# Weight sums of the last down projection moved into the second up projection, and gates by ScalarE's Silu

## The chip, the cores and the metric

The kernel runs on one core of a Trainium2 chip. A core has a matrix engine (TensorE, PE in the profile, its weight loads PEld), a vector engine (VectorE, DVE), a scalar engine for activation functions (ScalarE, ACT), a general engine (GpSimd, POOL) and an engine that issues transfers (SyncE, SP). SyncE, ScalarE and GpSimd can each issue DMA transfers. The metric is the time of one execution on the device in microseconds; the median of three runs is compared.

## The reference

The computation is a trunk of two layers on 512 tokens of width 1024, in float32. Each layer has a token mixer with three branches (an RWKV-7 recurrence, a chunked retention and a spatial gating unit), whose outputs are gated, summed and projected, and then a gated MLP with a causal convolution of width 3. A final RMSNorm ends it. The change touches the MLP only:

```python
def conv_ffn(h, w_up, conv_w, conv_b, w_down):
    S = h.shape[1]
    u = h @ w_up                                   # 1024 -> 2 x 2816
    up = jnp.pad(u, ((0, 0), (CONV_WIDTH - 1, 0), (0, 0)))
    c = conv_b
    for j in range(CONV_WIDTH):
        c = c + conv_w[j] * up[:, j:j + S]
    gate, val = jnp.split(c, 2, axis=-1)
    return (jax.nn.silu(gate) * val) @ w_down      # 2816 -> 1024

...
for l in range(DEPTH):                             # DEPTH = 2
    ...                                            # the mixer
    x = x + conv_ffn(rmsnorm(x, norm2_g[l]), ffn_w_up[l], ffn_conv_w[l], ffn_conv_b[l], ffn_w_down[l])
return rmsnorm(x, final_g)
```

## The kernel before

**Products.** Every large product is made of matmuls of 128x128 weights with 128x512 activations. For accuracy each operand is split into a high and a low part (`part` and `split`, lines 130 to 150: ScalarE copies the high part, line 139 or 148; VectorE subtracts, line 140 or 149), and each product takes three matmuls (`mm3`, line 152, issued at line 156). A unit of weights is 128x512, 256 KB. `load` (line 121) fetches units on SyncE's queue a few units ahead, in the order that a first pass over the program noted.

**Order.** The program is written once, in program order. A scheduler then orders each engine's instructions by their priority, which follows program order, and by a simulated time line. An instruction marked by `keep_in_program_order` is pinned behind the instruction that was written before it for the same engine. Each engine and each queue works in order, so an instruction that waits holds up those behind it. Tiles come from pools with a fixed number of buffers; a tile waits until the buffer's last user is done.

**Up projection (`ffn_up`, line 1058).** It makes 44 columns of 128 in pairs, column i for the gate and column 22 + i for the value, i from 0 to 21. One column is two units of weights and 24 matmuls into one of four accumulators (`acc`). VectorE takes the accumulator out with the norm's factor (line 1082, tile `fu`). ScalarE makes the first tap with the bias (line 1084), VectorE the other two (lines 1085 and 1086). For each pair ScalarE then makes a Tanh of half the gate (line 1090), and VectorE two products (lines 1091 and 1092), so the result is twice silu(gate) times the value; the factor of one half is applied behind the down projection. In layer 0 the result is split for the matmuls. In layer 1 `halves` (line 1101) combines each two results with four half-size VectorE instructions and two splits, and GpSimd's queue stores parts of it to DRAM (lines 1108, 1109, 1113). In layer 1 GpSimd's queue also turns the residual (line 1076) in the odd steps i below 17. The first three columns are computed before the norm's factor is known (`firstF`).

**Down projections.** Layer 0's (`ffn_down`, line 1117) makes 8 rows of 66 matmuls each. Layer 1's (`last`, line 1134) uses a seven-product scheme on 2x2 blocks. Four of the seven products need sums and differences of the four 128x512 blocks of a quad of weights; there are 11 quads, q = 0 to 10. It first goes through the quads with the products 4 to 7, 24 matmuls a quad, then through the products 1, 2 and 3.

**The weight sums (`presum`, line 237).** A quad is four loads on GpSimd's queue (line 253, tiles `pre` from tensor `wdt`), four VectorE subtractions or additions (lines 242 to 245) and four stores to DRAM (line 248, tensor `ts`), from where `load` reads them back in the last down projection. The table `PRE` says where a quad is loaded; it is summed at the next call. Quads 0 to 3 are loaded in layer 0's up projection at i = 2, 4, 6 and 8 into 16 tiles of the pool of activations (`fpre`), and quads 4 to 10 in layer 0's down projection, one for each of its first seven rows, into tiles of the general pool `u`. So all sums are done before layer 1 begins.

## Time and profile before

| | us |
|---|---|
| median of three runs | 1702.77 |
| lowest and highest run | 1701.46, 1706.15 |
| the profiled execution | 1701.58 |
| its span, first to last instruction | 1699.7 |
| TensorE busy in the span | 1687.0 |
| VectorE busy | 1233.1 |
| ScalarE busy | 799.9 |
| GpSimd busy | 240.8 |

The profile is of one execution. Its times are counted from the first instruction; the 1.9 us between its own time and its span lie before and behind. Matmuls are pipelined: each is listed with a length of some 390 ns, while the next starts earlier, so the pace has to be read from starts. VectorE and ScalarE overlap back-to-back instructions a little as well. A wait is put down to the instruction that released it. The line of an instruction is that of the statement, which can be in a helper; line 156 stands for almost all matmuls. Tiles are named without their numbers: `sh`, `sl` and `wh`, `wl` are the high and low parts of weights, `ah` of activations, `wr` the raw weights.

### The profile page before, as it was taken

What the parts mean: (1) busy time and instruction counts of PE and PEld (TensorE: products, weight loads), DVE (VectorE), ACT (ScalarE), POOL (GpSimd) and SP (SyncE); (2) the same over time, 40 slices, a digit from 0 to 9 for tenths busy, and PEclk for the clock granted to TensorE, in tenths of its full rate; (3) what the DMA queues carried; (4) which work ended last, traced back from release to release, by engine and by line L of the source; (5) the groups of instructions that cost most, each with busy time, mean ns of one, the idle gap of its engine ahead of it and who ended that gap; (6) DMA issues with size and microseconds to landing.
All of it is one profiled execution on the core that took longest, in us unless ns stands there. A gap on an engine that the chain in (4) does not pass through costs nothing.

```text
span 1699.7 us, 27885 instructions
## 1 busy us (share of the span) xinstructions
PE 1687.0 (99%) x10214; PEld 1379.7 (81%) x10214; DVE 1233.1 (73%) x2157; ACT 799.9 (47%) x1367; POOL 240.8 (14%) x336
## 2 busy tenths in 40 slices
PE   9999999999999999999999999999999999999998
PEld 7888777888888888888888888777888888887786
DVE  6887746578669887655568888455775698888776
ACT  6563433554355444433355644335542554444565
POOL 2121000003301200003321210000132022110000
PEclk9999999999999999999999999999999999999999
DMA  5236552524544532147743365525254443433774
GB/s 182 87 108 203 177 179 94 181 92 161 189 146 147 194 123 95 63 145 260 255 142 100 97 211 172 180 94 188 85 173 149 155 136 132 130 131 112 241 243 167
DMA packets 147768, 260.01 MB, mean 153 GB/s; under 512 B 19600, under 2 KB 39952, under 8 KB 147632
## 3 DMA queue, kind: packets, MB, share of 16 engines
q1 hardware_dynamic: 122960, 192.87, 35.2%
q0 software_dynamic: 15888, 49.95, 8.7%
q10 hardware_dynamic: 8784, 15.42, 2.6%
q8 instruction: 80, 1.31, 0.3%
q14 instruction: 56, 0.46, 0.1%
HBM read 212.94 MB, written 45.22 MB: 152 GB/s over the span
## 4 chain that ended last, share of the span: by engine, by line
PE 90%; DVE 4%; DMA 3%; issue 1%; ACT 1%; SPq 0%; ACTq 0%; DVEq 0%
PE acc L156 82%; PE sm L156 3%; PE sm L664 2%; DVE wl L140 1%; DMA wr<-wall 1%; PE sm L917 1%; PE sm L571 1%; DMA tr<-bkT 1%; DVE sl L140 0%; PE sm L1022 0%; ACT wh L139 0%; DVE cs L790 0%; DMA wr<-ts 0%; DVE TMP L788 0%; DMA x<-xT 0%
## 5 line engine op out<-in xcount | busy, mean ns | idle before, releaser
L156 PE MATMUL acc<-lo,sh 128*128 128x512 f32 x1108 | 431.8, 390 | 0.5 <-ACT sh L139 0.5
L156 PE MATMUL acc<-hi,sh 128*128 128x512 f32 x1108 | 431.9, 390 | 0.0
L156 PE MATMUL acc<-hi,sl 128*128 128x512 f32 x1108 | 430.3, 390 | 0.2 <-DVE sl L140 0.2
L139 ACT CAST sh<-wr 128x512 fp32r<-128x512 f32 (+1 forms) x375 | 228.3, 615 | 370.3 <-PE acc L156 217.6
L140 DVE TENSOR_TENSOR sl<-wr,sh 128x512 fp32r<-128x512 f32 (+1 forms) x375 | 254.5, 684 | 103.5 <-ACT sh L139 78.3
L140 DVE TENSOR_TENSOR wl<-wr,wh 128x512 fp32r<-128x512 f32 x238 | 166.5, 703 | 144.5 <-ACT wh L139 141.1
L139 ACT CAST wh<-wr 128x512 fp32r<-128x512 f32 x238 | 146.8, 619 | 244.4 <-PE acc L156 160.3
L156 PEld LDWEIGHTS acc<-lo,sh 128*128 128x128 f32 x1108 | 208.0, 188 | 45.0 <-ACT sh L139 1.2
L156 PEld LDWEIGHTS acc<-hi,sl 128*128 128x128 f32 x1108 | 208.0, 188 | 44.1 <-DVE sl L140 0.7
L156 PEld LDWEIGHTS acc<-hi,sh 128*128 128x128 f32 x1108 | 208.0, 188 | 43.1 <-issue 0.3
L156 PE MATMUL acc<-lo,wh 128*128 128x512 f32 x588 | 232.3, 395 | 0.3 <-DVE lo L215 0.2
L156 PE MATMUL acc<-hi,wl 128*128 128x512 f32 x588 | 229.8, 391 | 0.5 <-DVE wl L140 0.5
L156 PE MATMUL acc<-hi,wh 128*128 128x512 f32 x588 | 229.3, 390 | 0.0
L156 PEld LDWEIGHTS acc<-lo,wh 128*128 128x128 f32 x588 | 110.5, 188 | 25.5 <-DVE lo L215 1.5
L156 PEld LDWEIGHTS acc<-hi,wl 128*128 128x128 f32 x588 | 110.4, 188 | 25.4 <-DVE wl L140 1.5
L156 PEld LDWEIGHTS acc<-hi,wh 128*128 128x128 f32 x588 | 110.6, 188 | 22.5 <-issue 0.2
L156 PE MATMUL acc<-ah,sh 128*128 128x512 f32 x352 | 108.4, 389 | 0.0
L1084 ACT ACTIVATE cv<-fu,pc 128x512 f32<-128x512 f32 x88 | 71.6, 816 | 61.1 <-DVE fu L1082 59.8
L1082 DVE TENSOR_TENSOR fu<-acc,rsF 128x512 f32<-128x512 f32 x88 | 60.6, 688 | 39.8 <-PE acc L156 39.7
L156 PE MATMUL acc<-wl,hi 128*128 128x512 f32 x212 | 86.1, 406 | 0.0
L156 PE MATMUL acc<-wh,lo 128*128 128x512 f32 x212 | 82.8, 391 | 0.0
L156 PE MATMUL acc<-wh,hi 128*128 128x512 f32 x212 | 82.7, 390 | 0.0
(359 smaller groups left out, 2426.8 us busy)
## 6 DMA issues: line engine op xcount, KB each, us to landing
wr<-wall SPq DMA_DIRECT2D x488, 256.0 KB, 2.8
gd<-gth ACTq DMA_DIRECT2D x48, 256.0 KB, 3.0
gth<-gd POOLq DMA_DIRECT2D x48, 256.0 KB, 3.5
pre<-wdt POOLq DMA_DIRECT2D x44, 256.0 KB, 5.9
ts<-pre POOLq DMA_DIRECT2D x44, 256.0 KB, 2.8
wr<-ts SPq DMA_DIRECT2D x44, 256.0 KB, 3.9
wr<-wdn SPq DMA_DIRECT2D x40, 256.0 KB, 4.2
wr<-wdt SPq DMA_DIRECT2D x33, 256.0 KB, 3.6
```

The costliest lines, as they stand in the source:

```text
L139: self.kept(self.nc.scalar.copy(hi[:, :n], raw[:, :n]))
L140: self.kept(self.nc.vector.tensor_tensor(lo[:, :n], raw[:, :n], hi[:, :n], op=SUB))
L156: i = self.nc.tensor.matmul(*x, **y, **kw)
L571: i = T.matmul(pK[hv[1 - h], j, :], bk[hv[h], c, 1, :], x[hv[h], c, :], start=True, stop=True)
L664: po(T.matmul(o, l, r, start=start, stop=True, skip_group_check=True))
L917: po(T.matmul(X[h][:, i, :], lhsT, rhs, start=new[h], stop=stop, skip_group_check=True))
L1082: V.tensor_tensor(u, ps, self.rsF, op=MUL)
L1084: A.activation(t, u, AF.Identity, scale=self.p("cw2", j), bias=self.p("cb", j))
```

## The change

All eleven quads move into layer 1. A generator `sums` makes one quad in four steps: issue its four loads; nothing; two sums with their two stores; the other two sums with theirs. All of these are pinned in program order on VectorE and on GpSimd's queue. `presum` advances the generator by one step and does something in layer 1 only: after each column of the up projection with i below 20, after the first column of i = 20 (41 steps), and after the quads q = 0, 1 and 2 of the first pass of `last` (3 steps). So ten quads are done in the up projection; the eleventh is loaded at i = 20 and summed in `last`.

The tiles `pre` get a pool of their own with six buffers, four for a quad, so that two loads of the next quad find a free buffer and the other two wait for stores. [...] The 16 tiles of `fpre` and the 28 tiles of `u` are no longer taken in layer 0.

In both up projections ScalarE makes Silu of the gate in place of Tanh of half of it, and one VectorE instruction (twice silu, times the value) takes the place of two.

```diff
-PRE = {(0, "f", 2): 0, (0, "f", 4): 1, (0, "f", 6): 2, (0, "f", 8): 3, (0, "d", 0): 4, (0, "d", 1): 5, (0, "d", 2): 6, (0, "d", 3): 7,
-       (0, "d", 4): 8, (0, "d", 5): 9, (0, "d", 6): 10}
+RING = 4096
...
+        self.pp = tp("pp", 6)
...
-    def presum(self, l, stage, m):
...
+    def sums(self, l):
+
+        P, V, po = self.nc.gpsimd, self.nc.vector, self.tc.keep_in_program_order
+        for q in range(NFF // 2):
+            b = [self.pp.tile([128, 512], F32, name=self.nm("pre"), tag="pre") for _ in range(4)]
             for i, t in enumerate(b):
-                self.nc.gpsimd.dma_start(t, self.a["wdt"][0, 2 * q + i // 2][:, i % 2 * 512:i % 2 * 512 + 512])
-            self.pre.append((q, b))
+                po(P.dma_start(t, self.a["wdt"][l - 1, 2 * q + i // 2][:, i % 2 * 512:i % 2 * 512 + 512]))
+            yield
+            yield
+            for p, o, x, op in ((7, 3, 1, SUB), (5, 1, 0, SUB), (6, 0, 3, ADD), (4, 2, 0, SUB)):
+                po(V.tensor_tensor(b[o], b[o], b[x], op=op))
+                self.tsum[l, q, p] = self.dp.tile([128, 512], F32, name=self.nm("ts"))
+                po(P.dma_start(self.tsum[l, q, p], b[o]))
+                if p == 5:
+                    yield
+            yield
+
+    def presum(self, l):
+        if l == L - 1:
+            next(self.sum, None)
...
         first = self.firstF(l, (78, 79, 80), st, (3,))
-        if l == 0:
-            self.fpre = [[self.f(n="pre") for _ in range(4)] for _ in range(4)]
+        self.sum = self.sums(l)
         for i in range(NFF):
-            if l == 0 and i % 2 == 0 and 2 <= i <= 10:
-                self.presum(l, "f", i)
...
                 cs.append(t)
+                if i < 20 or i == 20 and j == i:
+                    self.presum(l)
             g, v = cs
             th = self.u(n="fth")
-            A.activation(th, g, AF.Tanh, scale=0.5)
-            V.scalar_tensor_tensor(th, th, 1.0, g, op0=ADD, op1=MUL)
-            V.tensor_tensor(th, th, v, op=MUL)
+            A.activation(th, g, AF.Silu)
+            V.scalar_tensor_tensor(th, th, 2.0, v, op0=MUL, op1=MUL)
...
-            self.presum(l, "d", m)
...
+            if q < 3:
+                self.presum(L - 1)
...
-        nc = _bacc.Bacc("TRN2", target_bir_lowering=False, num_devices=1)
+        nc = _bacc.Bacc("TRN2", target_bir_lowering=False, num_devices=1, dynamic_dma_scratch_size=RING)
```

More of the change, by code (lines that the diff above doesn't have):

```diff
@@ L123, in load @@
         raw = self.u(n="wr") if u[5] == "q" and self.nraw % 2 else self.wp.tile([128, 512], F32, name=self.nm("wr"), tag="wr", bufs=NRAW)
-        src = self.tsum[i] if name == "tsum" else self.a[name][l, i]
+        src = self.tsum[(l, *i)] if name == "tsum" else self.a[name][l, i]
         with self.tc.high_priority():
@@ L235, in trip @@
         return d
-    def presum(self, l, stage, m):
-        if self.pre:
-            q, b = self.pre.pop()
-            V = self.nc.vector
-            V.tensor_tensor(b[3], b[3], b[1], op=SUB)
-            V.tensor_tensor(b[1], b[1], b[0], op=SUB)
-            V.tensor_tensor(b[0], b[0], b[3], op=ADD)
-            V.tensor_tensor(b[2], b[2], b[0], op=SUB)
-            for p, t in zip((7, 5, 6, 4), (b[3], b[1], b[0], b[2])):
-                self.tsum[q, p] = self.dp.tile([128, 512], F32, name=self.nm("ts"))
-                self.nc.gpsimd.dma_start(self.tsum[q, p], t)
-        q = PRE.get((l, stage, m))
-        if q is not None:
-            b = self.fpre.pop(0) if stage == "f" else [self.u(n="pre") for _ in range(4)]
-            for i, t in enumerate(b):
-                self.nc.gpsimd.dma_start(t, self.a["wdt"][0, 2 * q + i // 2][:, i % 2 * 512:i % 2 * 512 + 512])
-            self.pre.append((q, b))
+    def sums(self, l):
+        P, V, po = self.nc.gpsimd, self.nc.vector, self.tc.keep_in_program_order
+        for q in range(NFF // 2):
+            b = [self.pp.tile([128, 512], F32, name=self.nm("pre"), tag="pre") for _ in range(4)]
+            for i, t in enumerate(b):
+                po(P.dma_start(t, self.a["wdt"][l - 1, 2 * q + i // 2][:, i % 2 * 512:i % 2 * 512 + 512]))
[11 more added lines that the diff above has]
+            next(self.sum, None)
     def norm_new(self):
@@ L326, in run @@
         self.con = self.cp.tile([128, NCC], F32, name="con")
-        self.pre, self.tsum = [], {}
+        self.tsum = {}
         self.rst = self.cp.tile([128, 512], F32, name="rst")
@@ L1144, in unit @@
             if p > 3:
-                return self.unit("tsum", 0, (q, p), 0)
+                return self.unit("tsum", L - 1, (q, p), 0)
             return self.unit("wdt", 0, 2 * q + (p > 1), 512 * (p == 3))
```

## The prediction

> **What bounds the kernel now.** I read the head of the page first, then the busy time by stretch, then the chain in order of time.

> ```profile
> span 1699.7 us, 27885 instructions
> PE 1687.0 (99%) x10214; PEld 1379.7 (81%) x10214; DVE 1233.1 (73%) x2157; ACT 799.9 (47%) x1367; POOL 240.8 (14%) x336
> PE 90%; DVE 4%; DMA 3%; issue 1%; ACT 1%; SPq 0%; ACTq 0%; DVEq 0%
> ```

> TensorE is busy for 99% of the span, so other work costs time only where it makes TensorE wait. The stretches that the change touches, from the view of busy time by stretch (after the length: PE, PEld, DVE, ACT, POOL busy with instruction counts, TensorE clock, DMA share, GB/s):

> ```profile
> 509.00:752.00 243.00, 243.00 (x1074) 201.28 (x1073) 196.36 (x310) 113.94 (x177) 15.03 (x28) 1.00 0.37 123
> 530.00:620.00 90.00, 90.00 (x399) 74.55 (x398) 79.96 (x127) 43.60 (x69) 15.03 (x28) 1.00 0.52 179
> 752.00:866.00 114.00, 114.00 (x505) 94.42 (x504) 61.14 (x97) 36.45 (x63) 34.35 (x64) 1.00 0.74 248
> 980.00:1142.00 162.00, 161.78 (x1785) 129.14 (x1785) 107.28 (x217) 65.60 (x118) 17.89 (x17) 1.00 0.52 167
> 1142.00:1262.00 120.00, 119.29 (x643) 98.27 (x639) 83.04 (x163) 59.84 (x111) 18.81 (x23) 1.00 0.44 143
> 1360.00:1380.00 20.00, 20.00 (x90) 16.56 (x89) 19.70 (x32) 11.41 (x17) 3.85 (x7) 1.00 0.41 133
> 1357.00:1572.00 215.00, 214.49 (x946) 176.93 (x944) 186.23 (x307) 100.67 (x157) 35.62 (x65) 1.00 0.39 128
> 1380.00:1560.00 180.00, 180.00 (x795) 149.02 (x794) 155.37 (x259) 83.61 (x132) 30.70 (x56) 1.00 0.39 129
> 1572.00:1600.00 28.00, 27.18 (x116) 21.46 (x116) 21.70 (x37) 13.20 (x23) 2.70 (x5) 1.00 0.62 190
> 1600.00:1620.00 20.00, 20.00 (x90) 16.52 (x90) 14.38 (x23) 12.81 (x24) 0.00 (x0) 1.00 0.96 330
> ```

> The first up projection is 509 to 752, the first down projection 752 to 866, the second up projection 1357 to about 1590, the last down projection after it. A busy PE can still be a slowed PE, so I checked the pace in the chain in order of time (start, length, what, count):

> ```profile
> 509.76 355.19 PE acc L156 x1567
> 1357.30 210.36 PE acc L156 x928
> ```

> 355.19/1567 and 210.36/928 both give 0.2267 us for one matmul. With VectorE 81% busy and 87% busy, with the sums there and without, TensorE steps at the same pace. A column (24 matmuls) is 5.44 us. The instructions of TensorE that waited between 1568 and 1606 (idle time in brackets):

> ```profile
> 1570.87 0.50 PE L156 MATMUL acc<-lo,sh 128*128 128x512 f32 x1 [0.51 <-ACT sh L139]
> 1572.35 0.50 PE L156 MATMUL acc<-hi,sl 128*128 128x512 f32 x1 [0.22 <-DVE sl L140]
> 1592.53 0.50 PE L156 MATMUL acc<-wl,ah 128*128 128x512 f32 x1 [0.41 <-DVE wl L140]
> 1598.78 0.50 PE L156 MATMUL acc<-sl,ah 128*128 128x512 f32 x1 [0.16 <-DVE sl L140]
> ```

> Together 1.30 us, always for the split of a weight. This seam between the second up projection and the last down projection is the only place under the change where TensorE waits for VectorE.

> **Part 1: the sums leave layer 0.** Removed there: 44 loads, 44 stores and 44 VectorE instructions.

> ```profile
> L242 DVE TENSOR_TENSOR pre<-pre,pre 128x512 f32<-128x512 f32 x11 | 7.6, 690 | 15.8 <-DMA pre<-wdt 15.8
> L248 POOL DMA_DIRECT2D ts<-pre x44 | 23.9, 542 | 194.8 <-DVE pre L242 169.3 <-DVE pre L245 8.4 <-DVE pre L243 6.0
> L253 POOL DMA_DIRECT2D pre<-wdt x44 | 23.4, 539 | 0.0
> ```

> and from the view of waits (in all, times, longest):

> ```profile
> DVE pre L242 <- DMA pre<-wdt: 15.8, 6, 3.3
> ```

> VectorE gets back 44 x 0.69 = 30 us and 15.8 us of waiting, GpSimd's queue 47 us of issues. All of it lies beside TensorE, which is full in both stretches (243.00 of 243, 114.00 of 114), so I take 0. What can follow is another order in layer 1's mixer. There TensorE's recorded idle is 0.22 + 0.71 us, the end below: -0.9. For the end above, compare the two layers' mixers, whose neighbours differ already:

> ```profile
> 199.21 1.27 PE sm L808 x83
> 414.55 1.42 PE sm L972 x13
> 1045.45 1.27 PE sm L808 x83
> 1261.37 1.42 PE sm L972 x13
> ```

> From L808 to L972 it is 215.34 us in layer 0 and 215.92 us in layer 1. The end above is +0.6.

> **Part 2: the sums and the gates in the second up projection.** One call a column makes one quad (four loads, four sums, four stores) every four columns, 21.8 us. Ten quads fit, the eleventh is loaded there and summed after q = 1 and 2 of the last down projection. Silu drops one VectorE instruction per gate.

> ```profile
> L1091 DVE SCALAR_TENSOR_TENSOR fth<-fth,cv 128x512 f32<-128x512 f32 x44 | 30.1, 684 | 0.2 <-ACT fth L1090 0.2
> L1090 ACT ACTIVATE fth<-cv 128x512 f32<-128x512 f32 x44 | 27.2, 618 | 0.5 <-DVE cv L1086 0.3
> ```

> VectorE: + 40 x 0.69 = 27.6, - 22 x 0.684 = 15.0, so +12.6 us over 44 columns, 0.29 us a column. In 1380 to 1560 VectorE was idle 24.6 us in 33 columns, 0.75 a column. That leaves 0.46 a column, about 20 us in the stage: VectorE goes from 86% to 92%. The nearest rows: in 530 to 620 VectorE had four quads and was 89% busy, and from 1360 to 1380 98%, and TensorE was full in both. I take 0; below nothing is to be had, since TensorE is full from 1380 to 1560; the end above is the first rival. In layer 0 the 22 dropped instructions are hidden by the same full TensorE.

> The DMA issues (count, size, median us from issue to landing):

> ```profile
> pre<-wdt POOLq DMA_DIRECT2D x44, 256.0 KB, 5.9
> ts<-pre POOLq DMA_DIRECT2D x44, 256.0 KB, 2.8
> wr<-wdn SPq DMA_DIRECT2D x40, 256.0 KB, 4.2
> ```

> GpSimd: 80 issues x 0.54 = 43 us more beside the 35.62 of 215 us now, so its queue has room; its order matters more. The loads of a quad are pinned behind the last store of the gates before, the sums two columns (10.9 us) after the call. Four issues and the landing (5.9 us) take 8.1 us, so they arrive in time by some 3 us, less when a store ahead of them waits for VectorE. Each store waits for its sum, and the next gate's two stores, for which L1114 waits, stand behind it; VectorE comes to the sum first, in the same order.

> The bus: 80 x 0.262 MB in 239 us is 88 GB/s on top of 128, together 216. In the first down projection it was 248 GB/s with the weights landing after 4.2 us, and TensorE full. Nothing.

> The smaller descriptor ring: the trace shows no wait for room. From below it is 0; from above, one more landing (5.9 us) per quad, which makes the sums 3 us late (first rival). Four loads were issued 0.54 us apart without a wait, so few are in flight, and I take 0. [...]

> Table loads of ScalarE, at the Tanh of the gates and at the Gelu of the mixer:

> ```profile
> L1090 ACT ACT_TABLE_LOAD x2: 1283/1283/1283, 518.6 to 1366.1; - x2
> L1004 ACT ACT_TABLE_LOAD x2: 1283/1283/1283, 334.6 to 1180.8; - x2
> ```

> Tanh had one per layer, after the Sqrt of the norm; Silu needs one too. If Silu's table lacked the copies of L139 and the Identity of L1084, each gate would cost two reloads, 22 x 2 x 1.28 = 56 us of ScalarE, 157 of 215 us.

> Tanh and Gelu ran among those copies with one load per stage, so I take 0. [...]

> **Part 3: the seam.** The last two gates give VectorE back 2 x 0.68 = 1.4 us. The eleventh quad puts in 4 x 0.69 = 2.8 us, in pairs, pinned between weight splits for which TensorE already waits, so a pair can be paid in full: net +1.4. Its four stores are 1.05 MB, 3.2 us of the bus at 330 GB/s, just before the loads of 1600 to 1620 (share 0.96), with TensorE full there. Ends: -1.3 (all four waits go) and 1.4 + 3.2 = +4.6. I take +1.4, since each recorded wait ends with a split and not with a load.

> **Sum.** 0 + 0 + 1.4. The profiled execution took 1701.58 us (span 1699.7 and 1.9 around it) and becomes 1703.0. It lies 1.2 below the median of 1702.77, so the median goes to 1704.2 us. About 0.3% (5.1 us) is what a measurement here tells from no change, as the three runs spread from 1701.46 to 1706.15.

> **Rivals.**
> Slower, VectorE falls behind in the second up projection: 6 of the 11 quads waited for their loads now, 15.8 us, 2.6 each, the longest 3.3 (the row of waits above). If all eleven wait, that is 29 to 36 us; about 20 are free, and TensorE pays 9 to 16: 1712 to 1719. It decides from 20/11 = 1.8 us a quad. For it: loads of one quad behind gate stores that wait for VectorE. Against: the 3 us in hand and the 89% row. An issue took 0.54 us, sixteen of them in the stretch where VectorE was 89% busy. [...]
> Slower, the seam pays bus and sums: 4.6 or more, 1707.4 and up, beyond 0.3% if a further split is late.
> Silu reloads tables at each gate: the splits queue behind 1.28 us loads; TensorE pays up to 56 us, 1759.
> Faster, the waits go: all of TensorE's recorded idle in 980 to 1262 and 1357 to 1600 is 0.22 + 0.71 + 0.51 + 0.82 = 2.3 us, 1700.5, still within 0.3%. More would need the end of the kernel, which the change doesn't touch.

> **How the numbers follow.** My forecast and the small gain, both within 0.3%: 0.71. VectorE behind: 0.13. The seam beyond 0.3%: 0.06. Tables: 0.03. Faster by over 0.3%, by a cause that I don't see: 0.07. So faster 0.07, same 0.71, slower 0.22. The range runs from 1700 (the gain, and the spread of runs) to 1712, where the first rival begins; left out are that rival, the tables and part of the faster case, about 0.2. Within the forecast alone it is 1701 to 1707.

> **What would show it.** Right: the pace stays 0.2267 in both long pieces of the chain; VectorE near 92% in 1380 to 1560; no wait for `pre` over 1 us; ten table loads; TensorE's waits at the seam 1 to 3 us in all. Wrong: waits of PE for `sh`, `sl` or accumulators inside the second up projection, long waits of VectorE for `pre` or of GpSimd for slots, or a mixer of layer 1 that differs by more than 1 us.

## The result, and the profile after

The changed kernel takes 1710.38 us (median of six runs, 1707.74 to 1711.77), the kernel before 1704.35 us on the same chip (1701.46 to 1706.15). The ratio is 1.0031, with a 95% interval from 1.0021 to 1.0042: slower by about 5.3 us, just at the bound of 0.3% that the prediction had set. The profiled execution took 1709.89 us, with a span of 1708.2 us against 1699.7. The head of its page:

```profile
span 1708.2 us, 27807 instructions
PE 1690.1 (99%) x10214; PEld 1382.0 (81%) x10214; DVE 1209.2 (71%) x2113; ACT 799.6 (47%) x1367; POOL 240.8 (14%) x336
PE 79%; DVE 7%; DMA 5%; issue 5%; ACT 2%; POOL 1%; SPq 1%; ACTq 0%; DVEq 0%; POOLq 0%
```

TensorE still fills 99% of the span, but the chain that ended last runs over it for 79% in place of 90%. From here on lines behind 240 are a few higher or lower than in the kernel before (L1081 takes the accumulator out, L1083 to L1085 make the taps, L1091 the Silu, L243, L247 and L249 load, add and store the sums).

Rows of the chain in order of time (start, length, what), by which the two executions can be laid side by side:

```profile
415.01 1.42 PE sm L974 x13
510.25 355.19 PE acc L156 x1567
1045.94 1.27 PE sm L810 x83
1262.67 1.42 PE sm L974 x13
1358.58 41.42 PE acc L156 x183
```

The changed kernel is 0.46 us late at the end of layer 0's mixer (415.01 against 414.55) and 0.49 late at 1045.94. So from layer 0's up projection, which has the same unbroken piece of 1567 matmuls in 355.19 us, to the start of layer 1 nothing was won or lost. Layer 1's mixer adds 0.8 (1.30 late at 1262.67), and the second up projection begins 1.28 late. The end is 8.5 late, so about 7.2 us are lost from the second up projection on. Its unbroken piece of 928 matmuls is cut down to 183. The busy time by stretch (after the length: PE, PEld, DVE, ACT, POOL busy, TensorE clock, DMA share, GB/s):

```profile
752.00:866.00 114.00, 114.00 (x505) 94.45 (x504) 43.36 (x69) 36.62 (x63) 4.33 (x8) 1.00 0.41 119
1380.00:1560.00 180.00, 178.64 (x785) 146.88 (x784) 158.60 (x268) 79.16 (x129) 67.83 (x126) 1.00 0.70 225
1577.00:1584.00 7.00, 6.44 (x16) 5.08 (x17) 3.26 (x6) 2.17 (x4) 1.11 (x3) 0.55 0.85 296
```

TensorE's waits between 1380 and 1610, and its matmuls behind the longest (idle time in brackets):

```profile
1496.68 0.50 PE L156 MATMUL acc<-lo,sh 128*128 128x512 f32 x1 [1.20 <-ACT sh L139]
...
1577.56 0.80 PE L156 MATMUL acc<-lo,sh 128*128 128x512 f32 x1 [3.57 <-ACT sh L139]
1578.15 0.63 PE L156 MATMUL acc<-hi,sh 128*128 128x512 f32 x1
1578.58 0.63 PE L156 MATMUL acc<-lo,sh 128*128 128x512 f32 x1
...
1582.85 0.63 PE L156 MATMUL acc<-hi,sh 128*128 128x512 f32 x1
...
1584.01 0.40 PE L156 MATMUL acc<-hi,sh 128*128 128x512 f32 x1
1584.24 0.39 PE L156 MATMUL acc<-hi,sl 128*128 128x512 f32 x1
...
1604.08 0.50 PE L156 MATMUL sm<-wl,ah 128*128 128x512 f32 x1 [0.34 <-DVE wl L140]
```

The waits are 5.1 us, against 1.30 before. Behind the wait of 3.57 us the matmuls come 0.43 us apart (1578.15, 1578.58, ...) and only by 1584 are they 0.23 apart again: the clock row says 0.55 there. From 1578.15 to 1582.85 eleven steps took 4.70 us where 2.49 was the pace, so these steps alone lost 2.2 us to the slow clock. The waits' 3.8 us more than before and these 2.2 make 6.0 of the 7.2 us; the rest lies in single long steps behind the first wait, near 1531 and at the edges of the slow stretch. About a third was lost early: from 1380 to 1560 ten matmuls fewer were made than before (785 against 795), which is 2.3 us at 0.2267 each. The mean granted clock was 0.997 or 0.998 in all six executions and 0.999 in the profiled one of the kernel before, so the others lost clock as well; where, their records do not show.

Why was `sh`, a cast of weights on ScalarE, late? Waits in 1380 to 1560, first of the kernel before, then of the changed one (in all, times, longest):

```profile
ACT sh L139 <- PE acc L156: 50.2, 38, 2.6
DVE fu L1082 <- PE acc L156: 10.0, 15, 1.6
ACT sh L139 <- DMA wr<-wall: 7.4, 3, 4.0
DVE sl L140 <- ACT sh L139: 1.7, 1, 1.7
```

```profile
ACT sh L139 <- DMA wr<-wall: 33.9, 18, 4.7
DVE sl L140 <- ACT sh L139: 15.2, 6, 4.2
ACT sh L139 <- PE acc L156: 6.8, 2, 4.7
DVE fu L1081 <- PE acc L156: 0.4, 1, 0.4
DVE pre L247 <- DMA pre<-wdt: 0.3, 1, 0.3
```

Before, VectorE and ScalarE waited for TensorE (10.0 and 50.2 us): both were ahead. After, VectorE hardly ever waits for TensorE (0.4 us): it runs behind. It does not wait for the blocks of the sums (0.3 us). It waits 15.2 us for ScalarE's casts (1.7 before), and those wait 33.9 us for weights to land. The weight loads issued in this stretch, before and after (count, size, median us from issue to landing):

```profile
wr<-wall SPq DMA_DIRECT2D x63, 256.0 KB, 2.6
wr<-wall SPq DMA_DIRECT2D x61, 256.0 KB, 3.6
```

### The profile page after: what moved, and what is told of

Same layout as the page of the kernel before. It is cut to its first block, busy times and chain, and to the rows that moved or that the text cites. A ratio compares the mean times of both kernels' runs of the same rounds, so it can differ in the third digit from the quotient of the medians.

```text
span 1708.2 us, 27807 instructions
## 1 busy us (share of the span) xinstructions
PE 1690.1 (99%) x10214; PEld 1382.0 (81%) x10214; DVE 1209.2 (71%) x2113; ACT 799.6 (47%) x1367; POOL 240.8 (14%) x336
## 4 chain that ended last, share of the span: by engine, by line
PE 79%; DVE 7%; DMA 5%; issue 5%; ACT 2%; POOL 1%; SPq 1%; ACTq 0%; DVEq 0%; POOLq 0%
PE acc L156 70%; PE sm L156 3%; PE sm L666 2%; DMA wr<-wall 2%; DVE sl L140 1%; PE sm L919 1%; DVE wl L140 1%; PE sm L573 1%; DVE fu L1081 1%; DVE pre L247 1%; DVE cv L1084 1%; DMA tr<-qkt 1%; POOL pre L243 0%; DVE cv L1085 0%; PE sm L1024 0%
## 5 line engine op out<-in xcount | busy, mean ns | idle before, releaser
L156 PE MATMUL acc<-lo,sh 128*128 128x512 f32 x1108 | 433.7, 392 | 4.8 <-ACT sh L139 4.8
L156 PE MATMUL acc<-hi,sh 128*128 128x512 f32 x1108 | 433.6, 391 | 0.0
L156 PE MATMUL acc<-hi,sl 128*128 128x512 f32 x1108 | 432.0, 391 | 0.2
L139 ACT CAST sh<-wr 128x512 fp32r<-128x512 f32 (+1 forms) x375 | 227.9, 615 | 334.0 <-PE acc L156 204.2
L140 DVE TENSOR_TENSOR sl<-wr,sh 128x512 fp32r<-128x512 f32 (+1 forms) x375 | 255.1, 685 | 147.0 <-ACT sh L139 88.7
L140 DVE TENSOR_TENSOR wl<-wr,wh 128x512 fp32r<-128x512 f32 x238 | 166.8, 703 | 137.7 <-ACT wh L139 132.7
L139 ACT CAST wh<-wr 128x512 fp32r<-128x512 f32 x238 | 146.7, 619 | 241.4 <-PE acc L156 158.1
L156 PEld LDWEIGHTS acc<-lo,sh 128*128 128x128 f32 x1108 | 208.8, 188 | 49.4 <-ACT sh L139 5.8
L156 PEld LDWEIGHTS acc<-hi,sl 128*128 128x128 f32 x1108 | 208.7, 188 | 44.9 <-DVE sl L140 0.9
L156 PEld LDWEIGHTS acc<-hi,sh 128*128 128x128 f32 x1108 | 208.8, 188 | 43.4 <-issue 0.3
L156 PE MATMUL acc<-lo,wh 128*128 128x512 f32 x588 | 232.3, 395 | 1.0 <-DVE lo L215 0.7
L156 PE MATMUL acc<-hi,wl 128*128 128x512 f32 x588 | 230.3, 392 | 0.6 <-DVE wl L140 0.6
L156 PE MATMUL acc<-hi,wh 128*128 128x512 f32 x588 | 229.4, 390 | 0.0
L156 PEld LDWEIGHTS acc<-lo,wh 128*128 128x128 f32 x588 | 110.5, 188 | 26.4 <-DVE lo L215 1.5
L156 PEld LDWEIGHTS acc<-hi,wl 128*128 128x128 f32 x588 | 110.4, 188 | 25.8 <-DVE wl L140 2.1
L156 PEld LDWEIGHTS acc<-hi,wh 128*128 128x128 f32 x588 | 110.5, 188 | 22.2 <-issue 0.2
L1083 ACT ACTIVATE cv<-fu,pc 128x512 f32<-128x512 f32 x88 | 71.6, 816 | 97.3 <-DVE fu L1081 97.3
L156 PE MATMUL acc<-ah,sh 128*128 128x512 f32 x352 | 108.3, 389 | 0.0
L156 PE MATMUL acc<-wl,hi 128*128 128x512 f32 x212 | 86.2, 406 | 0.0
L156 PE MATMUL acc<-wh,hi 128*128 128x512 f32 x212 | 82.9, 391 | 0.0
L156 PE MATMUL acc<-wh,lo 128*128 128x512 f32 x212 | 82.9, 391 | 0.0
L1081 DVE TENSOR_TENSOR fu<-acc,rsF 128x512 f32<-128x512 f32 x88 | 60.5, 688 | 31.3 <-PE acc L156 30.9
## 6 DMA issues: line engine op xcount, KB each, us to landing
wr<-wall SPq DMA_DIRECT2D x488, 256.0 KB, 2.8
gd<-gth ACTq DMA_DIRECT2D x48, 256.0 KB, 3.1
gth<-gd POOLq DMA_DIRECT2D x48, 256.0 KB, 3.5
pre<-wdt POOLq DMA_DIRECT2D x44, 256.0 KB, 4.5
ts<-pre POOLq DMA_DIRECT2D x44, 256.0 KB, 3.0
wr<-ts SPq DMA_DIRECT2D x44, 256.0 KB, 4.4
wr<-wdn SPq DMA_DIRECT2D x40, 256.0 KB, 2.7
wr<-wdt SPq DMA_DIRECT2D x33, 256.0 KB, 3.8
```

Of the source, the lines that this page charges most:

```text
L139: self.kept(self.nc.scalar.copy(hi[:, :n], raw[:, :n]))
L140: self.kept(self.nc.vector.tensor_tensor(lo[:, :n], raw[:, :n], hi[:, :n], op=SUB))
L156: i = self.nc.tensor.matmul(*x, **y, **kw)
L1081: V.tensor_tensor(u, ps, self.rsF, op=MUL)
L1083: A.activation(t, u, AF.Identity, scale=self.p("cw2", j), bias=self.p("cb", j))
```

## The experiments

Each kernel was timed against the kernel before on the same chip. Three theories stood at first, named in the expectations below, and a fourth came out of the first four runs.

**Silu alone.** In the kernel before:

```diff
-            A.activation(th, g, AF.Tanh, scale=0.5)
-            V.scalar_tensor_tensor(th, th, 1.0, g, op0=ADD, op1=MUL)
-            V.tensor_tensor(th, th, v, op=MUL)
+            A.activation(th, g, AF.Silu)
+            V.scalar_tensor_tensor(th, th, 2.0, v, op0=MUL, op1=MUL)
```

> The kernel before with Silu in both up projections, the weight sums left in layer 0. Theory 1 (VectorE's sums in the second up projection delay the casts of the activations, and ScalarE's casts of the next weights stand behind those; Silu only relieves VectorE): no slower than before, between -2 and +1 us, TensorE's wait of 0.51 us for sh near 1571 gone or smaller. Theory 3 (Silu brings another order that hurts): at least +3 us, with TensorE waits in 1490 to 1580.

Measured: 1700.99 us against 1702.07, ratio 0.9997 (0.9988 to 1.0006). TensorE's wait near 1571 shrank:

```profile
1569.92 0.50 PE L156 MATMUL acc<-lo,sh 128*128 128x512 f32 x1 [0.17 <-ACT sh L139]
```

Silu does no harm, and what it may bring is within the interval. Theory 3 falls.

**The sums with Tanh.** In the changed kernel the diff above the other way round.

> The changed kernel with Tanh and the two VectorE products put back; the sums stay in the second up projection. Theory 1: slower than the changed kernel by 2 to 10 us, since VectorE has 22 x 0.68 = 15 us more there, with more TensorE waits for sh and sl. Theory 2 (the 88 transfers make the weights late): like the changed kernel, within 2 us of 1710. Theory 3: back to the kernel before, 1704.

Measured: 1708.17 us against 1702.07, ratio 1.0040 (1.0027 to 1.0052), which is 6.8 us by the ratio. That is no clear step beyond the 1.0031 of the changed kernel, as theory 1 had asked for, and not the kernel before, as theory 3 had. The loss belongs to the move of the sums, whichever function makes the gates. It showed the same wait at the seam, 3.76 us, and the second row is VectorE's wait for casts in 1380 to 1560:

```profile
1574.71 0.80 PE L156 MATMUL acc<-lo,sh 128*128 128x512 f32 x1 [3.76 <-ACT sh L139]
```

```profile
DVE sl L140 <- ACT sh L139: 6.9, 8, 1.8
```

**No additions.** In the changed kernel, loads and stores kept:

```diff
             for p, o, x, op in ((7, 3, 1, SUB), (5, 1, 0, SUB), (6, 0, 3, ADD), (4, 2, 0, SUB)):
-                po(V.tensor_tensor(b[o], b[o], b[x], op=op))
```

> The changed kernel with the 44 VectorE additions of the weight sums left out (the loads and stores stay, so the last down projection multiplies by wrong weights). Theory 1: within 2 us of the kernel before (1704), no TensorE wait over 1 us in 1480 to 1580, no fall of the clock there. Theory 2: stays near 1710, with the wait of 3.6 us near 1574.

**No transfers.** In the changed kernel, additions kept:

```diff
-            b = [self.pp.tile([128, 512], F32, name=self.nm("pre"), tag="pre") for _ in range(4)]
-            for i, t in enumerate(b):
-                po(P.dma_start(t, self.a["wdt"][l - 1, 2 * q + i // 2][:, i % 2 * 512:i % 2 * 512 + 512]))
+            if q == 0:
+                six = [self.pp.tile([128, 512], F32, name=self.nm("pre"), tag="pre") for _ in range(6)]
+                for t in six:
+                    P.memset(t, 0.0)
+            b = [six[(4 * q + i) % 6] for i in range(4)]
...
-                self.tsum[l, q, p] = self.dp.tile([128, 512], F32, name=self.nm("ts"))
-                po(P.dma_start(self.tsum[l, q, p], b[o]))
+                self.tsum[l, q, p] = self.a["wdt"][l - 1, 2 * q + p % 2][:, 0:512]
```

> The changed kernel with the 44 loads and 44 stores of the weight sums left out: six tiles are zeroed once, VectorE makes its 44 additions on them, and the last down projection reads plain weights in place of the sums. Theory 1: stays at 1708 to 1712 with the wait of 3 to 4 us near 1574. Theory 2: back to 1704, with the bus share of 1380 to 1560 at 0.4 as before.

Measured: without additions 1702.99 us, ratio 1.0007 (0.9998 to 1.0016); without transfers 1701.99 us, ratio 1.0002 (0.9993 to 1.0011), both against 1702.07. Theory 1 had foreseen the first and failed on the second; theory 2 had foreseen the second and failed on the first. Neither the additions nor the transfers alone cost anything that can be told: it takes both. The stretch and its waits without additions:

```profile
1380.00:1560.00 180.00, 180.00 (x796) 149.08 (x795) 146.96 (x240) 82.61 (x132) 69.00 (x128) 1.00 0.70 232
```

```profile
DVE sl L140 <- ACT sh L139: 11.1, 8, 3.2
DVE fu L1080 <- PE acc L156: 5.4, 9, 1.1
```

And without transfers:

```profile
1380.00:1560.00 180.00, 180.00 (x796) 149.07 (x795) 165.01 (x277) 84.43 (x132) 31.00 (x57) 1.00 0.39 130
```

```profile
DVE fu L1082 <- PE acc L156: 3.2, 5, 0.9
DVE sl L140 <- ACT sh L139: 2.8, 5, 0.8
```

Without additions the bus is as full as in the changed kernel (0.70) and VectorE waits 11.1 us for casts of late weights, but has 33 us idle and stays ahead. Without transfers VectorE is busy for 165.01 of 180 us, the 92% of the prediction, but hardly ever waits for a cast and stays ahead with 15 us idle. This gave theory 4: VectorE's idle time is spent twice, by the additions and by waits for late weights, and with both it falls behind. The two are not a plain sum, though. With Tanh VectorE was busy for 169.21 of the 180 us, 10.6 us more than in the changed kernel, and the loss was not clearly larger; the waits for casts were 6.9 us there in place of 15.2. So the theory says when VectorE falls behind, and it does not give the size of the loss.

**Four raw weight tiles.** The weights are late only against the time at which they are issued, which is when one of three raw tiles comes free: in the changed kernel SyncE's queue waited 124.5 us between 1380 and 1560 for the splits that read them (L126 for `sl`, 55 times). A fourth lets each load start a unit earlier and changes nothing else that the theories speak of. The bus and the additions stay.

```diff
-NRAW = 3
-RING = 4096
+NRAW = 4
+RING = 2048
```

> The changed kernel with four raw weight tiles in place of three, so that each weight load is issued one unit earlier; the descriptor ring shrinks to 2048 bytes to make room. Theory 4 (new: VectorE's idle time is spent twice; the sums take one part, and the weights that land later beside the sums' transfers take the rest, because VectorE stands in its queue behind ScalarE's cast of a late weight, 15.6 us of such waits in 1380 to 1560; once VectorE runs a column late, the casts of the activations hold up the weights' casts): back to 1700 to 1705, with those waits under 5 us and no TensorE wait over 1 us in 1480 to 1580. Theory 1 alone (the sums' place in VectorE's order, not the late weights): stays at 1707 to 1711.

Measured: 1700.12 us against 1703.48, ratio 0.9979 (0.9970 to 0.9987): faster than both kernels. Stretch and waits:

```profile
1380.00:1560.00 180.00, 180.00 (x796) 149.05 (x795) 164.35 (x276) 83.07 (x132) 67.92 (x126) 1.00 0.71 232
```

```profile
ACT sh L139 <- PE acc L156: 45.5, 37, 2.1
ACT sh L139 <- DMA wr<-wall: 6.6, 3, 3.2
DVE sl L140 <- ACT sh L139: 2.5, 3, 1.7
```

The bus is as full as in the changed kernel (0.71), the weights land as late (median of 3.5 us against 3.6), the additions are all there (164.35 us), and yet the waits for casts fell from 15.2 to 2.5 us, ScalarE waits for TensorE again, and TensorE is full from 1380 to 1560. One wait of 1.21 us stays near 1570, a little more than the expectation allowed, and the clock held behind it (1.00 from 1560 to 1600):

```profile
1570.53 0.50 PE L156 MATMUL acc<-lo,sh 128*128 128x512 f32 x1 [1.21 <-ACT sh L139]
```

This confirms theory 4. The profiled execution had gained 1.0 us before the second up projection began, so the fourth tile helps in other places too. The smaller ring did no harm here either.

**The tenth quad later.** In the changed kernel:

```diff
-                if i < 20 or i == 20 and j == i:
+                if i < 18:
                     self.presum(l)
...
-            if q < 3:
+            if q < 4:
+                self.presum(L - 1)
                 self.presum(L - 1)
```

> The changed kernel with the tenth quad moved out of steps i = 18 and 19 of the second up projection into the last down projection, where quads ten and eleven take two steps at each of q = 0 to 3. If the sums just ahead of the seam make the wait near 1574 and the fall of the clock after it: 3 to 6 us faster than the changed kernel, 1703 to 1706, the waits near 1495 stay. If the backlog of VectorE built up before i = 18 makes it: less than 2 us faster.

Measured: 1711.42 us against 1703.48, ratio 1.0042 (1.0028 to 1.0056): not faster. In its profile the wait at the seam fell from 3.57 to 1.20 us, but the time moved to other places:

```profile
1501.68 0.50 PE L156 MATMUL acc<-lo,sh 128*128 128x512 f32 x1 [2.39 <-ACT sh L139]
1579.80 0.50 PE L156 MATMUL acc<-lo,sh 128*128 128x512 f32 x1 [1.20 <-ACT sh L139]
1613.27 0.62 PE L156 MATMUL acc<-wl,ah 128*128 128x512 f32 x1 [2.27 <-DVE wl L140]
1627.70 0.50 PE L156 MATMUL acc<-wl,ah 128*128 128x512 f32 x1 [1.63 <-DVE wl L140]
```

In the last down projection the sums stand ahead of weight splits that TensorE waits for, which is what the prediction had feared of the eleventh quad. The backlog near 1500 is still there, with a wait of 2.39 us. Whether the four sums just ahead of the seam lengthen the wait there is not shown: the next kernel still makes them just ahead of it (1565 to 1569), and its wait at the seam is 1.36 us. The profiled execution was the slowest of six (1715.54 us) and was 5.1 us behind the kernel before at the end of layer 1's mixer, so its lateness as a whole is not the MLP's.

**No pin on the additions.** In the changed kernel `po(V.tensor_tensor(...))` becomes `V.tensor_tensor(...)`.

> The changed kernel with the VectorE additions of the sums no longer pinned in program order (their loads and stores stay pinned). If the pin puts the sums ahead of more urgent work: 3 to 6 us faster than the changed kernel. Theory 4: within 3 us of the changed kernel, since VectorE has the same work and the same waits for late weights.

Measured: 1711.21 us against 1703.48, ratio 1.0041 (1.0029 to 1.0053). The pin is not the cause: in this profile VectorE still waited 11.2 us for casts of late weights, and TensorE 3.45 us near 1499:

```profile
1499.39 0.50 PE L156 MATMUL acc<-hi,sl 128*128 128x512 f32 x1 [3.45 <-DVE sl L140]
```

**Four raw tiles with the sums in layer 0.** The kernel before with Silu, with the ring passed on as in the change, and:

```diff
-NRAW = 3
+NRAW = 4
+RING = 4096
```

> The kernel before with Silu, four raw weight tiles and the descriptor ring of 4096 bytes; the sums stay in layer 0. The ring alone costs nothing by all theories. Theory 4: nothing in the MLP waits for weights, so within 2 us of the kernel with Silu alone (1701); a little faster where the mixers wait for weights.

Measured: 1702.02 us against 1703.48, ratio 0.9986 (0.9976 to 0.9997). Together with the kernel without additions (1.0007), which has the ring of 4096 and all 88 transfers, it shows no cost of the ring. It also shows that a gain does not need the move of the sums. How much of it is the fourth tile's and how much Silu's (0.9997 alone), and whether the move adds anything to it (0.9979 against 0.9986), the intervals don't tell apart.

## Why the prediction was right or wrong

The measured ratio of 1.0031 is 5.3 us, against +1.4 forecast and 5.1 for the bound. The direction was right, the time lies within the range, the size was too small by a factor of almost four, and the result sits on the bound between the forecast and the slower cases. That the direction was right is luck: the +1.4 was to come from the eleventh quad's sums at the seam, which cost next to nothing, and the loss came from a step that the working had put at nothing.

Part 1 held: removing the sums from layer 0 gave nothing. In the first down projection VectorE fell from 61.14 to 43.36 us and the bus from 248 to 119 GB/s, and TensorE was full in both. Layer 1's mixer came out 0.8 us later, a little past the end of 0.6. From 1045.94 to 1262.67 it is 216.73 us, against 215.92 before; in the eight other profiles the same piece took from 214.56 to 218.69, so 0.8 us can't be told from such differences.

Part 2 failed in one step: the bus, which was given as "Nothing". The transfers came about as the working had them (225 GB/s, where it had 216, at a share of 0.70), and the weights landed after 3.6 us (2.6 before), sooner than the 4.2 us of the row that was taken as cover. But that row, the first down projection, had a VectorE busy for 61 of 114 us. There late weights cost idle time that nobody needed. Here they cost 15.2 us of VectorE's time through ScalarE's casts, and the idle time left in the same 33 columns was 15 us, by the prediction's own 0.46 us a column and by the kernel without transfers alike. The other row, 89% busy with four quads in layer 0, had a bus of 0.52. Neither row had both loads at once, and each of the two charges was held against the whole of the same reserve.

So the first rival's place was right (VectorE behind in the second up projection), and its price had the right reserve, but its wait was the wrong one. VectorE waited 0.3 us for `pre`: the 3 us in hand for the loads of a quad were enough, and GpSimd's order held up nothing. 15.2 us between 1380 and 1560 came from `sh`. TensorE's listed waits for it lie in two places only, near 1496 and just ahead of the seam, and the loss was 7.2 us in the profile and not 9 to 16.

Part 3 put the loss at the right place with the wrong sums. The four additions of the eleventh quad cost little: the only wait listed there is 0.34 us, near 1604. The wait of 3.57 us comes just ahead of the seam. There ScalarE stands in its queue at the casts of the activations (`ah`) of step 19, which come ahead of the next three casts of weights:

```profile
1574.40 0.81 ACT L1083 ACTIVATE cv<-fu,pc 128x512 f32<-128x512 f32 x1 [3.83 <-DVE fu L1081]
1575.12 0.60 ACT L148 CAST ah<-wh 128x512 fp32r<-128x512 f32 x1
1576.37 0.62 ACT L148 CAST ah<-fth 128x512 fp32r<-128x512 f32 x1 [0.65 <-DVE fth L1114]
1576.89 1.66 ACT L139 CAST sh<-wr 128x512 fp32r<-128x512 f32 x3
...
1571.54 0.69 DVE L247 TENSOR_TENSOR pre<-pre,pre 128x512 f32<-128x512 f32 x1
1572.14 0.69 DVE L1092 SCALAR_TENSOR_TENSOR fth<-fth,cv 128x512 f32<-128x512 f32 x1
1572.74 0.69 DVE L247 TENSOR_TENSOR pre<-pre,pre 128x512 f32<-128x512 f32 x1
```

ScalarE waited 3.83 us for VectorE's accumulator of the next column, and VectorE had run the tenth quad's sums before that. ScalarE's wait stands in its queue ahead of weights that needed nothing more than their cast. That the clock would fall behind such a wait was not in the working at all; it is at least 2.2 us of the 7.2.

Of the signs named, the second long piece (183 matmuls in place of 928), the VectorE share (88% and not 92%, because it waited) and TensorE's waits at the seam (3.57 and 0.34 us, 3.9 in all and not 1 to 3) showed the prediction wrong; `pre` and the table loads (still one per up projection at the Silu, 1.28 us each) showed it right. The steps on Silu, the tables, the ring and GpSimd's issues stand. An issue of a load took 0.539 us and one of a store 0.546 between 1357 and 1572 (0.539 and 0.542 in the kernel before). No run shows how many transfers the ring, which the diffs set by `RING`, has room for; what the runs show is no cost of it, with a ratio of 1.0007 at 4096 bytes and all 88 transfers and of 0.9979 at 2048.

## What to carry to other kernels

A reserve of idle time is spent by everything that draws on it: add up the work that moves to an engine and the waits that its own transfers will give that engine, and look for a cover row that carries both at once. The sum says where to look and not what it costs. When an engine in the middle of a chain stops waiting for the bottleneck and begins to wait for its inputs, it has fallen behind, even while the bottleneck still looks full: here VectorE's waits for TensorE went from 10.0 to 0.4 us and those for casts from 1.7 to 15.2, with TensorE busy for 178.64 of 180 us. Then a deeper prefetch can be worth more than moving the work: here one more raw tile turned 1.0031 into 0.9979, and with the sums left in layer 0 it is 0.9986.

## What the runs showed of the hardware

TensorE's clock fell in some waits of 2.3 to 3.8 us. Behind 3.57 us the matmuls came 0.43 us apart in place of 0.23 for about 6 us, and the mean granted clock was 0.55 from 1577 to 1584; the kernel with Tanh showed the same behind 3.76 us (0.62 from 1575 to 1582), and the kernel without the pin behind 3.45 us (0.76 from 1499 to 1506). A wait of 1.20 us left the pace alone. In between it is not the length alone that decides. In the kernel with the tenth quad later, 2.27 us was followed by a slow stretch (0.66 from 1613 to 1618) and 2.39 us was not (1.00 from 1502 to 1509).

```profile
1573.12:1576.53 3.41, 0.87 (x4) 0.38 (x2) 3.28 (x8) 1.48 (x3) 2.16 (x5) 1.00 0.53 195
1576.53:1579.95 3.42, 2.39 (x6) 1.92 (x7) 3.42 (x6) 2.02 (x4) 1.58 (x3) 0.50 0.80 272
1579.95:1583.36 3.41, 3.41 (x10) 2.65 (x9) 0.06 (x1) 0.62 (x1) 0.00 (x0) 0.50 0.91 323
1583.36:1586.77 3.41, 3.41 (x17) 2.79 (x16) 2.70 (x4) 2.30 (x5) 0.00 (x0) 1.00 0.35 97
```

In the kernel with the tenth quad later the wait of 2.39 us (1499.29 to 1501.68) lies across two windows, the first two rows, and the wait of 2.27 us lies in one, the third row; the fourth is the window behind it:

```profile
1497.45:1500.87 3.42, 1.85 (x9) 1.19 (x7) 3.23 (x7) 1.68 (x3) 3.32 (x7) 1.00 0.66 206
1500.87:1504.28 3.41, 2.47 (x9) 1.71 (x10) 3.38 (x6) 1.80 (x4) 2.62 (x5) 1.00 0.97 317
1610.09:1613.50 3.41, 1.14 (x6) 0.64 (x5) 3.31 (x6) 0.62 (x1) 2.14 (x4) 1.00 1.02 391
1613.50:1616.92 3.42, 3.42 (x9) 2.67 (x9) 2.12 (x4) 1.37 (x3) 0.00 (x0) 0.50 1.05 407
```

In these rows the clock was halved behind the windows in which TensorE was busy for 0.87 and 1.14 us, and not behind those with 1.85 and 2.47. The window of the changed kernel with the wait of 1.20 us had 2.09 us of it (1494.61 to 1498.03), and the clock stayed at 1.00. It came back in the changed kernel behind the first window that TensorE filled, the third of its rows. So of the two waits of the kernel with the tenth quad later the shorter one cost clock and the longer one did not, and what the rows show between them is how they lay in the windows.
